# A four-layer block and a retrieval layer on one core: where the rows of the last 128 tokens are made, and how a gate becomes a row

## The chip, the cores and the metric

One NeuronCore of a Trainium2 chip runs the whole program. The metric is device time in microseconds; three executions of the kernel before took 2742.12 to 2751.5 us, median 2744.99. TensorE does matrix products, VectorE and ScalarE work on rows of 128 partitions, GpSimd (POOL) and SyncE (SP) here only issue DMAs. Profiled instructions are named by engine and by line of the kernel: L1447 is line 1447.

## The reference

512 tokens of width 1024 pass four mixer layers and then a block whose last part is a retrieval layer. All of the change lies in that part and in what follows it:

```
def peer_ffn(h, wq, sub_keys, expert_u, expert_v):          # h: (1, 512, 1024)
    ...
        q = (xb @ wq).reshape(PEER_BLOCK, PEER_HEADS, 2, PEER_HALF)
        s = jnp.einsum('thpd,hpkd->thpk', q, sub_keys)
        ...                                     # 8 heads choose 16 of 16,384 experts each
        g = jax.nn.softmax(best_s, axis=-1)
        act = jax.nn.gelu(jnp.einsum('thkd,td->thk', expert_u[experts], xb))
        wgt = g * act
        return jnp.einsum('thk,thkd->td', wgt, expert_v[experts])

    x = x + g2 * peer_ffn(h2, ...)              # g2: one gate of 1024 numbers for all tokens
    return rmsnorm_2(x, final_g)
```

## The kernel before

`peer()` computes this layer in two ways side by side. For tokens 0 to 319 it multiplies them by all 16,384 experts, 128 at a time: the *score part* `s_part()` (24 matmuls of 320 columns, lines 268 to 270 inside `gemm_t`, then a gelu on ScalarE, L1235) and, with the gates put in by VectorE (L1538), the *value part* `value_part()` (16 matmuls of 512 columns over three token blocks, L1483, L1484, L1486). Each of the 128 weights of `p_u` and of `p_v` (512 KB) is loaded by SP (L59), and split into a high and a low piece by ScalarE (L72, `whi`) and VectorE (L77, `wlo`). Raw weights have two or three buffers, split ones four.

For the other 192 tokens it gathers single experts' rows from DRAM: 64 tokens in halves (two partitions for each token, `two=True`) and the last 128 tokens one to a partition. POOL issues 384 gathers of 512 KB (L1456) into a ring of eight buffers. For a row of `p_u`, VectorE multiplies it with the token's normed row, kept in `hn` with one token on each partition, and sums (L1463); for a row of `p_v` it adds it with its weight to `ysum_h` or `ysum` (L1473). `hn` can hold one set of tokens: `hidden(True)` makes the 64 tokens' rows in front of the loop, and `hidden(False)` those of the last 128 when `consume()` has done the last product of the first kind. Both turn columns into rows by 16 matmuls with an identity (L1447) into two banks and two copies on ScalarE (L1448).

The last loop of `peer()` has 128 steps (L1525 on). A step loads the gates' columns `gr` (L1533, L1534), forms `wx` (L1538, L281, L282), consumes gathers, does a value part, for 21 <= i < 116 a score part for a later step, and issues up to four gathers by the table `CLOCK`. At i = 114 `last_rows()` makes `rw`, the two rows that the end needs on every partition: `final_g` by a broadcast DMA (L1491), and the gate `ada[:, 5]`, which lies in columns, by eight transposes into two banks (L1495) and two copies (L1496). `final(t)` multiplies a block's sums with the gate (L1515), adds the residual `y` (loaded at L1506, added at L1516), and norms it (L1518 to L1521). The value sums hold six of the eight PSUM banks through the loop, three of them in the pool of five whose other two serve all score parts, `hidden` and `last_rows`.

The code gives the order in which work is written down; a scheduler then orders the instructions of each engine by its own estimates, and an engine takes its list in order. So an edit in one place may move instructions in others. Loads of SP wait in SP's list in the same way, for a free buffer.

Of the kernel before, what the change touches and what calls it, by code (L numbers as in the profile page):

```python
# [10 lines left out]
F32 = mybir.dt.float32  # L11
# [3 lines left out]
AF = mybir.ActivationFunctionType  # L15
# [4 lines left out]
D = 1024  # L20
# [68 lines left out]
def program(ctx, tc, A, out, upto=99, dbg=None):  # L89
    nc = tc.nc  # L90
    V, SC, G, PE = nc.vector, nc.scalar, nc.gpsimd, nc.tensor
# [19 lines left out]
    dram = ctx.enter_context(tc.tile_pool(name="dram", bufs=1, space=bass.MemoryType.DRAM))  # L111

    def big(shape, dt, name):
        return bigp.tile(shape, dt, name=name, tag="big")

    def bank(shape=(128, S), pool="a"):
        return psp[pool].tile(list(shape), F32, name="bank" + pool, tag="bank" + pool)
# [4 lines left out]
    def tmp(shape, dt=F32, name="w2"):  # L122
        return w2.tile(shape, dt, name=name, tag="w2")
# [66 lines left out]
    ident = const.tile([128, 128], F32, name="ident")  # L190
# [716 lines left out]
    ada = const.tile([128, 6, KD], F32, name="ada")  # L907
# [294 lines left out]
    def peer(nrm, lp):  # L1202
# [6 lines left out]
        NG = ND // 32  # L1209
        gsp = dram.tile([32, 128, NG - 1, 128], F32, name="gsp")  # L1210
        gsl = dram.tile([32, 128, 128], F32, name="gsl")
        identr = lp.tile([128, 128], F32R, name="identr")
        V.tensor_copy(identr, ident)
        iota = lp.tile([128, 128], F32, name="iota")
# [88 lines left out]
        for m in range(16):  # L1303
# [8 lines left out]
            x = tmp([128, NT, 128])  # L1312
# [109 lines left out]
        hn = lp.tile([128, D], F32, name="hn")  # L1422
# [12 lines left out]
        def hidden(two):  # L1435

            for a in range(2):
                p = bank([128, 512])
                xs = [x[:, 4 * a:4 * a + 4, ND:ND + HALF] if two else x[:, 4 * a:4 * a + 4, ND + HALF:] for x in (nrm.h, nrm.l)]
                if two:  # L1440
                    twice = [tmp([128, 4, 2, HALF], F32R) for _ in xs]
                    for y, x in zip(twice, xs):
                        V.tensor_copy(y, x[:, :, None, :].to_broadcast([128, 4, 2, HALF]))
                    xs = [y.rearrange("p k a t -> p k (a t)") for y in twice]
                for k in range(4):
                    for i, x in enumerate(xs):
                        PE.matmul(p[:, k * 128:(k + 1) * 128], x[:, k], identr, start=i == 0, stop=i == 1)  # L1447
                SC.activation(hn[:, a * 512:(a + 1) * 512], p, AF.Copy)  # L1448
        act = lp.tile([128, 128], F32, name="act")
        ysum_h = lp.tile([128, D], F32, name="ysum_h")  # L1450
        order = [(two, p, n) for two in (True, False) for p in range(2) for n in range(HALF if two else 128)]
# [7 lines left out]
        def consume(two, p, n, u):  # L1459
            a, y, g = act[:, n:n + 1], ysum_h if two else ysum, gate_h if two else gate  # L1460
            last = g.shape[1] - 1
            if p == 0:
                V.tensor_tensor_reduce(u, u, hn, 1.0, 0.0, OP.mult, OP.add, a)  # L1463
                if n == last:
                    x = act[:, :last + 1]
                    SC.activation(x, x, AF.Gelu_apprx_tanh)
                    V.tensor_tensor(x, x, g, OP.mult)
                    if two:
                        hidden(False)
            elif n == 0:  # L1470
                V.tensor_scalar(y, u, a, None, OP.mult)
            else:
                V.scalar_tensor_tensor(y, u, a, y, OP.mult, OP.add)  # L1473
# [14 lines left out]
        def last_rows():  # L1488

            rw = big([128, 2, D], F32, "rw")  # L1490
            nc.sync.dma_start(rw[:, 1], A["final_g"].to_broadcast([128, D]))  # L1491
            for a in range(2):
                p = bank([128, 512])
                for k in range(4):
                    PE.transpose(p[:, k * 128:(k + 1) * 128], ada[:, 5, 4 * a + k:4 * a + k + 1].to_broadcast([128, 128]), ident)  # L1495
                SC.activation(rw[:, 0, a * 512:(a + 1) * 512], p, AF.Copy)  # L1496

            sel = lp.tile([128, 3 * HALF], F32, name="sel", tag="cand0")
            V.memset(sel, 0.0)
            V.tensor_tensor(sel[:, HALF:2 * HALF], ident[:, :HALF], ident[:, HALF:], OP.add)  # L1500
            return rw, sel

        def final(t):
# [18 lines left out]
            nc.sync.dma_start(out[0, t * 128:(t + 1) * 128], y[:, 1])  # L1522

        hidden(True)
        ring = [big([128, 4 * D], F32, "it") for _ in range(2)]  # L1525
        ring = [r[:, k * D:(k + 1) * D] for r in ring for k in range(4)]
        step, used, held, fetched = 0, 0, [], []
        clock = np.cumsum([CLOCK[(i >= MORE) + (i >= 128 - AHEAD)] for i in range(128)])
        for i in range(128):
# [16 lines left out]
            while fetched and fetched[0][0] <= i - LAG:  # L1546
                consume(*fetched.pop(0)[1:])
                used += 1
            if i == 114:
                rw, sel = last_rows()  # L1550
# [90 lines left out]
    if upto > 5:  # L1641
        with layer_pools(5) as lp:
            peer(nrm, lp)
# [119 lines left out]
```

## Time and profile before

| | before |
|---|---|
| median of three runs | 2744.99 us (2742.12 to 2751.5) |
| the profiled execution | 2749.09 us, of which the span from first to last instruction is 2747.0 us |
| TensorE, weight loads, VectorE, ScalarE, POOL busy | 95%, 81%, 79%, 47%, 20% of the span |
| moved by DMA | 653.67 MB, mean 238 GB/s |
| the last loop's DMA rate, slices 29 to 39 of 40 | 381 to 408 GB/s |

All rows come from the profiled execution. Times are microseconds from the start of its span. A busy time is the sum of an engine's instructions; a matmul's end is modelled, so it is the distance from one start to the next that tells how fast TensorE goes. Idle time is given with the instruction whose end finished it. `PEclk` is the clock granted to TensorE, as a share of the full one. "DMA" is the mean busy share of the 16 DMA engines; it can read a little over 1.

### The profile page before, as it was taken

Reading aid. Unit: us, or ns where it says so; the run is one execution under the profiler, and the core shown is the slowest. Engines: PE = TensorE matmul, PEld = TensorE weight load, DVE = VectorE, ACT = ScalarE, POOL = GpSimd, SP = SyncE. Lnnn points to the kernel's source line nnn. Section 1 sums busy time; section 2 is a strip of 40 time slices with the busy share of each in tenths; the row PEclk is TensorE's granted clock in tenths of the full one; section 3 lists DMA queues with packets and bytes.
Section 4 is the critical chain, followed back from the end, with each engine's and each line's share of the span. In section 5 each row is a group of like instructions: output and inputs, shape, how many; then the busy total and the mean of one; then the engine's idle time right before and its main releaser. Section 6 shows DMA issues by size and latency. Waiting matters only on the chain.

```text
span 2747.0 us, 40757 instructions
## 1 busy us (share of the span) xinstructions
PE 2610.9 (95%) x14379; PEld 2216.9 (81%) x14379; DVE 2174.8 (79%) x5296; ACT 1295.7 (47%) x2269; POOL 548.6 (20%) x431
## 2 busy tenths in 40 slices
PE   8999999999999999999999998889989999999988
PEld 7888888777767877897787788877879888888876
DVE  8975987756776777664435899788999899999998
ACT  5333455736775434445622346574444343444433
POOL 0000000000000000000000000005665666665661
PEclk9999999999999999999999999999999999999999
DMA  8773522142227886433345267779999999999996
GB/s 265 252 262 119 177 81 66 49 130 80 93 66 269 281 297 230 142 101 102 111 156 155 70 199 249 252 237 386 403 408 405 381 403 401 408 407 400 390 392 243
DMA packets 239788, 653.67 MB, mean 238 GB/s; under 512 B 23264, under 2 KB 80736, under 8 KB 239456
## 3 DMA queue, kind: packets, MB, share of 16 engines
q1 hardware_dynamic: 132640, 400.63, 41.7%
q0 software_dynamic: 61488, 223.90, 21.2%
q10 hardware_dynamic: 45456, 26.54, 3.3%
q8 instruction: 113, 1.85, 0.3%
q14 instruction: 91, 0.75, 0.1%
HBM read 583.29 MB, written 67.67 MB: 237 GB/s over the span
## 4 chain that ended last, share of the span: by engine, by line
PE 44%; DVE 22%; DMA 13%; issue 10%; POOL 5%; ACT 5%; ACTq 1%; SPq 0%; POOLq 0%; DVEq 0%
PE bankg L268 8%; PE bankg L269 8%; PE bankg L270 8%; POOL it L1456 5%; DVE wlo L77 4%; DMA wraw<-in_p_v_dram 3%; DMA wraw<-in_p_u_dram 3%; DVE ysum L1473 2%; PE bankg L428 2%; DVE it L1463 2%; PE bankg L430 2%; PE bankg L429 2%; DMA preraw<-in_p_u_dram 2%; PE bankg L543 2%; ACT whi L72 2%
## 5 line engine op out<-in xcount | busy, mean ns | idle before, releaser
L72 ACT ACTIVATE whi<-wraw 128x1024 fp32r<-128x1024 f32 (+1 forms) x491 | 515.3, 1051 | 806.0 <-PE bankg L269 220.6
L77 DVE TENSOR_TENSOR wlo<-wraw,whi 128x1024 fp32r<-128x1024 f32 (+2 forms) x448 | 541.3, 1209 | 206.1 <-ACT whi L72 199.6
L268 PE MATMUL bankg<-XH,whi 128*128 128x512 f32 x1032 | 408.9, 397 | 19.6 <-ACT whi L72 8.6
L270 PE MATMUL bankg<-XH,wlo 128*128 128x512 f32 x1032 | 405.3, 393 | 0.0
L269 PE MATMUL bankg<-XL,whi 128*128 128x512 f32 x1032 | 405.3, 393 | 0.0
L75 POOL DMA_DIRECT2D wlo<-lod x43 | 23.1, 538 | 1764.2 <-DVE vi L1319 1225.4
L268 PE MATMUL banka<-XH,whi 128*128 128x320 f32 x1024 | 320.8, 313 | 6.3 <-ACT whi L72 4.9
L270 PE MATMUL banka<-XH,wlo 128*128 128x320 f32 x1024 | 319.3, 312 | 4.6 <-DVE wlo L77 4.3
L269 PE MATMUL banka<-XL,whi 128*128 128x320 f32 x1024 | 317.6, 310 | 0.0
L268 PEld LDWEIGHTS bankg<-XH,whi 128*128 128x128 f32 x1032 | 195.7, 190 | 64.3 <-issue 11.9
L1463 DVE CUSTOM_DVE_ANT_0 it<-it,hn 128x1024 f32<-128x1024 f32 x192 | 229.9, 1217 | 6.9 <-DMA it<-in_p_urows_dram,idx 6.9
L270 PEld LDWEIGHTS bankg<-XH,wlo 128*128 128x128 f32 x1032 | 195.3, 189 | 41.3 <-DVE wlo L77 0.8
L269 PEld LDWEIGHTS bankg<-XL,whi 128*128 128x128 f32 x1032 | 195.5, 189 | 39.7 <-DVE XL L245 0.3
L268 PEld LDWEIGHTS banka<-XH,whi 128*128 128x128 f32 x1024 | 193.7, 189 | 13.6 <-ACT whi L72 5.1
L270 PEld LDWEIGHTS banka<-XH,wlo 128*128 128x128 f32 x1024 | 193.4, 189 | 8.6 <-DVE wlo L77 8.1
L1456 POOL DMA_INDIRECT it<-in_p_urows_dram,idx x128 | 179.9, 1406 | 94.1 <-DVE act L1463 71.4
L1456 POOL DMA_INDIRECT it<-in_p_v_dram,idx x128 | 173.8, 1358 | 113.7 <-DVE ysum L1473 102.4
L269 PEld LDWEIGHTS banka<-XL,whi 128*128 128x128 f32 x1024 | 193.6, 189 | 3.6
L428 PE MATMUL bankg<-whi,XH 128*128 128x256 f32 x576 | 165.1, 287 | 2.1 <-ACT XH L244 1.2
L430 PE MATMUL bankg<-whi,XL 128*128 128x256 f32 x576 | 164.1, 286 | 1.4 <-DVE XL L245 1.4
L429 PE MATMUL bankg<-wlo,XH 128*128 128x256 f32 x576 | 163.8, 285 | 0.0
L1473 DVE SCALAR_TENSOR_TENSOR ysum<-it,act,ysum 128x1024 f32<-128x1024 f32 x127 | 162.2, 1277 | 0.0
(513 smaller groups left out, 5835.5 us busy)
## 6 DMA issues: line engine op xcount, KB each, us to landing
wraw<-in_p_u_dram SPq DMA_DIRECT2D x128, 512.0 KB, 6.9
wraw<-in_p_v_dram SPq DMA_DIRECT2D x128, 512.0 KB, 7.2
wraw<-in_a_in_dram SPq DMA_DIRECT2D x64, 512.0 KB, 4.9
adaw<-in_ada_w_dram SPq DMA_DIRECT2D x48, 512.0 KB, 5.8
lod<-prelo SPq DMA_DIRECT2D x43, 512.0 KB, 5.9
wlo<-lod POOLq DMA_DIRECT2D x43, 512.0 KB, 5.5
gsp<-stage ACTq DMA_DIRECT2D x9, 2048.0 KB, 12.5
gr<-gsp SPq DMA_DIRECT2D x32, 576.0 KB, 8.3
```

The source lines that it names most:

```text
L72: nc.scalar.activation(h, t, AF.Copy)
L77: nc.vector.tensor_tensor(l, t, h.bitcast(F32), OP.subtract)
L268: PE.matmul(ps, a, xh[:, k, :], start=k == 0, stop=False)
L269: PE.matmul(ps, a, xl[:, k, :], start=False, stop=False)
L270: PE.matmul(ps, b, xh[:, k, :], start=False, stop=k == kk - 1)
L428: PE.matmul(ps, a, wh, start=k == 0, stop=False)
L429: PE.matmul(ps, a, wl, start=False, stop=False)
L430: PE.matmul(ps, b, wh, start=False, stop=k == len(blocks) - 1)
L543: PE.matmul(po[64 * a:64 * a + 64, b * 128:], v(m)[:, b, d:d + 64], xs[a][:, o:o + 128 * (NT - b)], start=b == 0, stop=b == 2)
L1456: G.indirect_dma_start(out=u, out_offset=None, in_=rows, in_offset=bass.IndirectOffsetOnAxis(ap=(idx_h if two else idx)[:, n:n + 1], axis=0))
L1463: V.tensor_tensor_reduce(u, u, hn, 1.0, 0.0, OP.mult, OP.add, a)
L1473: V.scalar_tensor_tensor(y, u, a, y, OP.mult, OP.add)
```

## The change

Two results are made in another place or way. First, `hidden(False)` is called right behind `hidden(True)`, in front of the loop. As `hn` still holds the 64 tokens' rows then, it copies its two halves into scratch tiles and SP stores them to a DRAM tile `hnd`. Where `consume()` called it, POOL now loads `hn` from `hnd`. Second, the gate row is not made by transposes: SP writes the columns of `ada[:, 5]` as one row to a DRAM tile `gate_row` at the start of `peer()`, and `last_rows()` loads it onto all partitions by a broadcast DMA.

```
+        hnd = dram.tile([128, D], F32, name="hnd")
+        gate_row = dram.tile([1, D], F32, name="gate_row")
+        nc.sync.dma_start(gate_row.rearrange("o (k p) -> p (o k)", p=128), ada[:, 5])
...
-                SC.activation(hn[:, a * 512:(a + 1) * 512], p, AF.Copy)
+                x = hn[:, a * 512:(a + 1) * 512] if two else tmp([128, 512])
+                SC.activation(x, p, AF.Copy)
+                if not two:
+                    nc.sync.dma_start(hnd[:, a * 512:(a + 1) * 512], x)
...
                     if two:
-                        hidden(False)
+                        nc.gpsimd.dma_start(hn, hnd)
...
-            for a in range(2):
-                p = bank([128, 512])
-                for k in range(4):
-                    PE.transpose(p[:, k * 128:(k + 1) * 128], ada[:, 5, 4 * a + k:4 * a + k + 1].to_broadcast([128, 128]), ident)
-                SC.activation(rw[:, 0, a * 512:(a + 1) * 512], p, AF.Copy)
+            nc.sync.dma_start(rw[:, 0], gate_row.to_broadcast([128, D]))
...
         hidden(True)
+        hidden(False)
```

Line numbers of the changed kernel are higher by three to six behind the first new lines: L1463 is L1469 there, L1538 is L1541, L1483 is L1489.

Beside the edited lines the scheduler orders three places anew. The first is VectorE at the start of the last loop; `w_...` are scratch tiles, the rows ahead of the first gather product are shown. Before:

```order
L77 TENSOR_TENSOR wlo<-wraw,whi 128x1024 x2
L282 TENSOR_TENSOR wx<-w_18408,wx 128x320
L282 TENSOR_TENSOR wx<-w_18455,wx 128x320
L1538 TENSOR_TENSOR w_18583<-sgb,gr 128x320
L77 TENSOR_TENSOR wlo<-wraw,whi 128x1024
L1538 TENSOR_TENSOR w_18630<-sgb,gr 128x320
L1538 TENSOR_TENSOR w_18672<-sgb,gr 128x320
L1538 TENSOR_TENSOR w_18707<-sgb,gr 128x320
L1538 TENSOR_TENSOR w_18744<-sgb,gr 128x320
L1463 ISA it,act<-it,hn 128x1024
L1463 ISA act 128x1
```

and with the change:

```order
L1431 COPY gr<-stage 128x128
L77 TENSOR_TENSOR wlo<-wraw,whi 128x1024 x6
L1469 ISA it,act<-it,hn 128x1024
L1469 ISA act 128x1
L1469 ISA it,act<-it,hn 128x1024
L1469 ISA act 128x1
L1469 ISA it,act<-it,hn 128x1024
L1469 ISA act 128x1
L1541 TENSOR_TENSOR w_18298<-sgb,gr 128x320
L1260 CAST w_18326<-vi 128x256
L1541 TENSOR_TENSOR w_18350<-sgb,gr 128x320
L282 TENSOR_TENSOR wx<-w_18298,wx 128x320
```

Before, all of the first steps' products L1538 stand ahead of the first gather product (L1463), and so does the end of `choose(TD)`, some 30 rows higher. Now six splits of weights (L77) and three gather products (L1469) stand ahead of the first of either.

The second is TensorE at i = 114, at the end of a score part. Before:

```order
L268 MATMUL banka<-XH,whi 128x320
L269 MATMUL banka<-XL,whi 128x320
L270 MATMUL banka<-XH,wlo 128x320
L1495 MATMUL banka<-ident,ada 128x128 x4
L1483 MATMUL bankg<-whi,wx 128x512
L1484 MATMUL bankg<-wlo,wx 128x512
L1486 MATMUL bankg<-whi,wx 128x512
L1483 MATMUL bankg<-whi,wx 128x512
```

and with the change:

```order
L268 MATMUL banka<-XH,whi 128x320
L269 MATMUL banka<-XL,whi 128x320
L270 MATMUL banka<-XH,wlo 128x320
L1489 MATMUL bankg<-whi,wx 128x512
L1490 MATMUL bankg<-wlo,wx 128x512
L1489 MATMUL bankg<-whi,wx 128x512
L1492 MATMUL bankg<-whi,wx 128x512
```

The four transposes between score part and value part are gone, and so are four more behind the value part's fourth matmul. The last two score parts, which before stand behind 163 further value matmuls in the list, now follow within 16 value matmuls each.

The third is SP at the end of the loop. Before:

```order
L59 DMA wraw<-in_p_v_dram 128x1024 x3
L1533 DMA gr<-gsp 128x1152
L1534 DMA gr<-gsl 128x128
L59 DMA wraw<-in_p_v_dram 128x1024 x9
L1491 DMA rw<-in_final_g_dram 128x1024
L1506 DMA y<-x_14423 128x1024 x4
L1522 DMA out_dram<-y 128x1024 x4
```

and with the change:

```order
L59 DMA wraw<-in_p_v_dram 128x1024 x3
L1536 DMA gr<-gsp 128x1152
L1537 DMA gr<-gsl 128x128
L59 DMA wraw<-in_p_v_dram 128x1024 x2
L1497 DMA rw<-in_final_g_dram 128x1024
L1498 DMA rw<-gate_row 128x1024
L59 DMA wraw<-in_p_v_dram 128x1024
L1508 DMA y<-x_14423 128x1024
L59 DMA wraw<-in_p_v_dram 128x1024 x2
L1536 DMA gr<-gsp 128x1152
L1537 DMA gr<-gsl 128x128
L59 DMA wraw<-in_p_v_dram 128x1024 x4
```

The loads of `rw` (now two) and the first of `y` stood behind the last weight and now stand in front of seven and of six weights. The buffers for `rw` and for the first `y` are those of the normed columns `XH` and `XL`, which the last score part reads.

## Rows read from the trace of the kernel before

**Rows 1.** the page, section 1 and the DMA row of section 2 (tenths)
```profile
PE 2610.9 (95%) x14379; PEld 2216.9 (81%) x14379; DVE 2174.8 (79%) x5296; ACT 1295.7 (47%) x2269; POOL 548.6 (20%) x431
...
DMA  8773522142227886433345267779999999999996
```

**Rows 2.** stretches: start:end, length, busy us (count) by engine, PEclk, DMA, GB/s
```profile
1872.00:1890.00 18.00, 17.73 (x77) 14.21 (x77) 17.76 (x29) 6.33 (x12) 11.59 (x8) 1.00 1.04 404
...
2020.00:2040.00 20.00, 11.66 (x56) 10.24 (x55) 18.30 (x20) 8.46 (x14) 10.37 (x10) 0.74 1.03 408
...
2040.00:2140.00 100.00, 100.00 (x552) 89.83 (x551) 95.90 (x99) 41.43 (x69) 59.88 (x46) 1.00 1.03 406
...
2140.00:2160.00 20.00, 20.00 (x114) 18.11 (x114) 15.91 (x18) 5.82 (x9) 11.11 (x9) 1.00 0.88 335
...
2160.00:2660.00 500.00, 487.01 (x2620) 427.26 (x2618) 470.33 (x619) 203.59 (x329) 318.36 (x229) 1.00 1.02 401
...
2660.00:2680.00 20.00, 13.95 (x62) 11.35 (x61) 19.41 (x22) 7.99 (x14) 12.56 (x10) 0.83 1.01 386
...
2700.00:2720.00 20.00, 20.00 (x105) 17.34 (x104) 19.74 (x23) 9.59 (x17) 1.22 (x1) 1.00 0.60 212
```

**Rows 3.** waits in 1880 to 2740: us in total, times, longest us
```profile
ACT whi L72 <- DMA wraw<-in_p_v_dram: 196.3, 95, 8.3
...
ACT whi L72 <- DMA wraw<-in_p_u_dram: 133.6, 70, 5.1
```

**Rows 4.** TensorE's rows: start, length, line, tiles, count [idle <- who], 2021 to 2040
```profile
2021.90 0.31 PE L270 MATMUL banka<-XH,wlo 128*128 128x320 f32 x1
...
2025.80 0.33 PE L1447 MATMUL banka<-identr,XH 128*128 128x128 f32 x1 [3.58 <-ACT sgb L1235]
...
2036.55 0.40 PE L1483 MATMUL bankg<-whi,wx 128*128 128x512 f32 x1
...
2038.87 0.31 PE L268 MATMUL banka<-XH,whi 128*128 128x320 f32 x1
...
2039.74 0.31 PE L268 MATMUL banka<-XH,whi 128*128 128x320 f32 x1
```

**Rows 5.** stretches at the mid-loop stop, columns as in rows 2
```profile
2026.00:2036.00 10.00, 5.25 (x21) 4.67 (x21) 10.00 (x11) 4.61 (x9) 5.48 (x5) 0.51 1.03 410
```

**Rows 6.** TensorE's rows at the stop ahead of the tail
```profile
2662.20 0.31 PE L270 MATMUL banka<-XH,wlo 128*128 128x320 f32 x1
...
2670.14 1.12 PE L1495 MATMUL banka<-ident,ada 128*128 128x128 f32 x4 [5.37 <-ACT sgb L1235]
...
2675.53 0.39 PE L1483 MATMUL bankg<-whi,wx 128*128 128x512 f32 x1
```

**Rows 7.** VectorE's rows at the start of the last loop
```profile
1842.20 0.49 DVE L1538 TENSOR_TENSOR w<-sgb,gr 128x320 f32<-128x320 f32 x1 [2.86 <-DMA gr<-gsp]
...
1850.56 0.23 DVE L1562 TENSOR_SCALAR idx<-ei 128x128 int32<-128x128 int32 x1
...
1872.03 1.23 DVE L77 TENSOR_TENSOR wlo<-wraw,whi 128x1024 fp32r<-128x1024 f32 x1 [0.42 <-ACT whi L72]
...
1874.78 1.22 DVE L1463 CUSTOM_DVE_ANT_0 it<-it,hn 128x1024 f32<-128x1024 f32 x1
```

**Rows 8.** TensorE's row of the first value matmul
```profile
1868.63 0.45 PE L1483 MATMUL bankg<-whi,wx 128*128 128x512 f32 x1
```

**Rows 9.** TensorE's row of the last value matmul
```profile
2730.91 0.40 PE L1484 MATMUL banka<-wlo,wx 128*128 128x512 f32 x1
```

**Rows 10.** VectorE's rows behind the last gather: its next and its last
```profile
2716.04 1.22 DVE L77 TENSOR_TENSOR wlo<-wraw,whi 128x1024 fp32r<-128x1024 f32 x1
...
2741.80 1.28 DVE L1521 SCALAR_TENSOR_TENSOR y<-y,rs_yb,rw 128x1024 f32<-128x1024 f32 x1
```

**Rows 11.** SyncE's queue: the first load of rw
```profile
2708.90 0.33 SPq L1491 DMA_DIRECT2D rw<-in_final_g_dram  x1
```

## The prediction

> **What bounds the kernel now.** I read the page first, then the table of stretches, then the waits of the last loop, and then single rows where TensorE stands. By the page TensorE is busy 95% of the span [rows 1], but that is a mean over all stages. What the change touches lies in the last loop, from 1868.6 us [rows 8] to the end, so its stretches decide [rows 2]. The reader is to see three nearly full resources there. The DMA engines stand at a share of 1.01 to 1.04 and 386 to 408 GB/s from 1872 on, but for 2140 to 2160 (0.88, 335). VectorE works 470.33 of the 500 us from 2160. TensorE's busy time is modelled, so I count matmuls instead: a step is 16 matmuls of the value part at 0.232 us (ten of them lie between 2036.55 and 2038.87 [rows 4]) and 24 of the score part at 0.146 (six between 2038.87 and 2039.74, with rounding), 7.2 us for 40. The 552 matmuls of 2040 to 2140 make 99.4 of 100 us: TensorE is at its peak. The 2620 of 2160 to 2660 make 472 of 500: it is starved for about 5%, though its busy time reads 487.
>
> By the Trainium skill ("Perfetto Trace Analysis", Identifying the Most-Contended Engine) a matmul's busy share is a poor measure of the distance from the peak, and the busy share of the weight loads a better one. By the former (97%) TensorE would set the pace; by the latter, 427 us where the peak of 89.83 per 100 would be 449, it is starved for 5%, as the count says.
>
> Who starves it is seen in the waits [rows 3]: ScalarE's split of a weight (L72) waits 196.3 and 133.6 us for weights to land. So over the long stretch the DMA engines pace the loop, and TensorE only here and there.
>
> **What goes: the stop in mid-loop.** The 16 matmuls of L1447 stand behind a score part whose bank ScalarE has not emptied; the first starts at 2025.80 after 3.58 us of idle time [rows 4], and then the granted clock is 0.51 in 2026 to 2036 [rows 5], the lower of its levels. Between the start of the last score matmul before it (2021.90) and that of the next score part (2038.87) lie 16.97 us, with one value part of 16 x 0.232 = 3.7 us in them. TensorE loses 13.3 us. **The stop ahead of the tail** is alike: eight transposes (L1495) in two banks, the second four after 5.37 us of idle time; from 2662.20 to 2675.53 are 13.3 us for one value part [rows 6]. It loses 9.6. Together 22.9.
>
> What is late next there? Without L1447 a value part comes first, which needs no new bank and takes 3.7 us; the next score part needs the bank that ScalarE gives free at 2025.80, 3.9 us after 2021.90. So nearly all of the stop goes.
>
> But is it on the path? During the first stop the DMA engines ran at 1.03 and 408 GB/s [rows 2], so what paces the loop lost nothing. Behind it TensorE is at its peak until 2140 and starved again from 2160: the buffers (four split weights, two or three raw ones) had swallowed the 13 us. I cost that gain at nothing. Behind the second stop TensorE doesn't recover; it runs to its last value matmul at 2730.91 [rows 9]. But VectorE works 19.41 and 19.74 of 20 us around the tail [rows 2], and its last row ends the span but for the store [rows 10]. So a gain there counts only as far as VectorE's list behind the last gather gets shorter.
>
> **What is added.** The normed rows go to DRAM and back, 0.52 + 0.52 MB: at 408 GB/s 2.6 us of the DMA engines. The write stands on SP's queue behind six weights and ahead of reloads for step 12 and later; the read on POOL's queue between two gathers, where it waits for the last product of the first kind, while the ring's gathers behind it wait for VectorE's same row anyway: nothing. One load of `rw` and the first of `y` went out at 2708.90 and later [rows 11], where the DMA engines are at 0.60 [rows 2]; now SP issues them, and the second load of `rw`, among the last nine weights, in the saturated stretch: 3 x 0.52 = 1.57 MB, 3.8 us. VectorE's new order at the change of gather kind may spare the dip of 2140 to 2160: (408 - 335) / 408 x 20 = 3.6 us. In all 2.6 + 3.8 - 3.6 = +2.8 us of DMA time.
>
> By the Trainium skill ("DMA: Bandwidth & Descriptors", Issuing engines are not separate DMA queues) loads from SP and POOL share the same 16 engines; the trace agrees, with 408 GB/s as the most that both queues reach. Were POOL's queue a path of its own, the read back would be free and the sum +1.5. The rule speaks against a trip by DRAM in this loop: by it alone, with nothing won on TensorE, the time would be 2745 + 2.8 = 2748, the upper edge of the forecast's own range.
>
> SP's write of 1,024 single elements, about 1,065 us into the span by its place in SP's order, has no row of its kind. From below it costs nothing: the page's slice there, the sixteenth (1030 to 1099 us), shows DMA at 6 tenths [rows 1], and the row isn't read for another 1,600 us. From above it holds the two weight loads behind it for one stop like those of rows 4, 3.6 us. I take 0, as that slice is far from the 9 tenths of the last loop.
>
> **What moves** is the start of the loop. Before, VectorE did the rest of `choose(TD)` and four products L1538 from 1842.20 to 1850.79, then eight more L1538 and five L282 between the first six L77, and the first gather product at 1874.78 [rows 7]; the first value part began at 1868.63 [rows 8]. Now six L77 stand first, of which the last ran until 1873.3 [rows 7]; three gather products of 1.2 us; two L1538, a cast and L282, 1.6 us: the first value part comes at about 1878.5, up to 2 us earlier if weights land earlier, as SP now issues six of them ahead of four reloads of 0.16 MB. TensorE loses 8 to 10 us, I take 9. And 8.6 + 13 x 0.45 = 14 us of VectorE's work move into the loop; it has 30 us idle in the long stretch alone [rows 2]. The first gather product itself comes 1.5 us earlier, so the ring of eight gathers doesn't stop sooner. DMA time lost: 0, if the gathers fill the gap, to 4 us, the weights' share of 9 (in the long stretch 229 gathers [rows 2] go with 2620 / 40 x 2 = 131 weights, 0.36 of the loads; rounded up).
>
> **Sum.** The last gather lands 2.8 to 6.8 us later. Behind the last gather's sum VectorE needs 27 us (2716.04 to 2743.1 [rows 10]); two L77, two L1538 and two L282 of these, 4.4 us, now stand ahead of it. And the eight gathers of the ring, 10 us of VectorE's work when the last one landed, may be less behind with TensorE not stopped: 0 to 8 us. So from 2.8 - 4.4 - 8 = -9.6 to 6.8 - 4.4 = +2.4, the middle -3.6. The sum is made against the profiled 2749.09: 2745.5. That execution lies 4.1 above the median of 2744.99 in all its parts as far as I can tell, so I take the difference over to the median: **2741**.
>
> **The rivals.**
> *TensorE sets the pace.* For it: its peak in 2040 to 2140, and the value matmuls in a row to 2730.91. Then 22.9 - 9 = 14 us are won: 2731. Against it: 472 of 500 us.
> *The late start decides.* If the raw weights and the ring are full before VectorE's first gather product, the DMA engines stand until the first value part frees a buffer, 9 us that a saturated loop can't make good, and 2.8 of the bytes: 2745 + 11.8 = 2757. It decides once loads stop for more than about 5 us after 1872. Against it: 404 GB/s in 1872 to 1890 [rows 2], with VectorE's first product at 1874.78.
> *The change doesn't do what it says at the tail:* SP holds `rw` until the last score part frees its buffer, seven weights behind it, and the stop comes back as a wait for weights: 5.4 us once more [rows 6], 2750.
>
> **How the numbers follow.** Forecast 0.47 (2741, its own range 2735 to 2748), TensorE sets the pace 0.25 (2731), late start 0.20 (2757), held queue 0.08 (2750). What a measurement of this kernel can tell from no change is about 0.3%, 8.2 us: below 2736.8 is faster, above 2753.2 slower. Faster: 0.25 and 0.05 of the forecast's lower edge, 0.30. Slower: 0.18 and 0.02, 0.20. Within: 0.50. The range, 2730 to 2757, leaves out about 0.1 on each side.
>
> **What would show it.** Right: no idle time over 1 us of TensorE at the two places, and a count of matmuls behind the first that now falls short of the peak; the DMA share as before; the first value part near 1878; the last gather 3 to 7 us later, and VectorE's rows behind its sum near 22 us. Wrong: a loop that ends 14 us earlier with more than 408 GB/s (TensorE paced), a hole in the DMA share between 1872 and 1890 (late start), or a wait for weights behind `rw`.

## The result, and the profile after

The change makes the kernel slower: 1.0069 of the time before (95% interval 1.0054 to 1.0085); medians 2762.9 and 2744.99 us. 2741 was forecast, 2730 to 2757 the range. One of the seven executions of the change took 7164.13 us and is left out of the ratio. The profiled execution's span is 2756.1 us, 9.1 longer than that of before; it was the fastest of the six others, so the profile shows less of the loss than the medians do.

The page of the kernel after; the rows answer to [rows 1]:

```profile
span 2756.1 us, 40696 instructions
...
PE 2611.6 (95%) x14371; PEld 2215.4 (80%) x14371; DVE 2172.1 (79%) x5296; ACT 1300.1 (47%) x2267; POOL 561.9 (20%) x432
...
DMA  7773522132227896433344267779999999999996
```

TensorE and VectorE do the same work as before (their busy times differ by less than 3 us) in a longer span. The stretches of the last loop, with the columns of [rows 2] (start:end, length, then TensorE, weight loads, VectorE, ScalarE, POOL busy with counts, clock, DMA share, GB/s):

```profile
1872.00:1890.00 18.00, 14.61 (x52) 11.73 (x53) 15.38 (x38) 7.00 (x15) 7.76 (x6) 0.75 0.98 331
1890.00:1950.00 60.00, 59.55 (x256) 47.61 (x255) 57.72 (x122) 25.45 (x45) 29.29 (x22) 1.00 1.01 383
1950.00:2020.00 70.00, 70.00 (x376) 61.99 (x375) 64.35 (x102) 28.59 (x47) 42.47 (x31) 1.00 1.01 388
2020.00:2040.00 20.00, 20.00 (x111) 17.95 (x110) 18.84 (x29) 8.51 (x15) 14.70 (x11) 1.00 1.03 407
2040.00:2140.00 100.00, 98.22 (x534) 86.29 (x532) 95.92 (x99) 42.11 (x66) 60.40 (x46) 1.00 1.03 408
2140.00:2160.00 20.00, 18.53 (x104) 16.44 (x103) 18.98 (x21) 7.74 (x12) 12.97 (x9) 1.00 1.03 408
2160.00:2660.00 500.00, 481.48 (x2597) 422.13 (x2596) 472.52 (x620) 204.68 (x327) 332.34 (x231) 1.00 1.02 402
2660.00:2680.00 20.00, 19.84 (x107) 17.34 (x106) 20.00 (x22) 8.69 (x13) 13.57 (x10) 1.00 1.03 407
2680.00:2700.00 20.00, 13.40 (x56) 10.47 (x55) 14.65 (x17) 5.46 (x10) 9.24 (x9) 0.91 1.03 409
2700.00:2720.00 20.00, 17.46 (x74) 13.47 (x73) 19.41 (x24) 7.91 (x15) 7.42 (x6) 1.00 0.95 358
```

Three of these stretches before, which [rows 2] leave out:

```profile
1890.00:1950.00 60.00, 59.71 (x256) 47.77 (x255) 54.70 (x88) 27.14 (x46) 30.43 (x25) 1.00 1.03 405
1950.00:2020.00 70.00, 69.48 (x380) 61.54 (x378) 69.32 (x109) 28.97 (x49) 50.77 (x35) 1.00 1.03 405
...
2680.00:2700.00 20.00, 20.00 (x87) 16.11 (x86) 19.36 (x20) 7.46 (x12) 10.45 (x10) 1.00 1.03 406
```

Three things are to be seen. The mid-loop stop is gone (2020 to 2040: 20.00 us busy, 11.66 before), the clock stays at 1.00 there (0.74 before), and the next stretch now counts 534 matmuls instead of 552: TensorE is starved at once, as forecast. The start is worse: 331 GB/s in 1872 to 1890 (404 before), with the granted clock at 0.75 behind TensorE's wait for its first value part, then 383 and 388 where 405 was measured before. Against those rates the three stretches miss 73 x 18 + 22 x 60 + 17 x 70 = 3.8 MB, 9.4 us at 405 GB/s. And the tail is no longer full: TensorE's 13.40 of 20 us in 2680 to 2700 and 17.46 in 2700 to 2720, both 20.00 before.

**The start**, VectorE's rows ahead of the loop, which answer to [rows 7], and TensorE's first value matmul, which answers to [rows 8]:

```profile
1840.02 0.23 DVE L1431 COPY gr<-stage 128x128 f32<-128x128 f32 x1 [1.57 <-ACT stage L1408]
...
1855.45 2.36 DVE L77 TENSOR_TENSOR wlo<-wraw,whi 128x1024 fp32r<-128x1024 f32 x2 [15.20 <-ACT whi L72]
```

```profile
1875.39 0.80 PE L1489 MATMUL bankg<-whi,wx 128*128 128x512 f32 x1 [6.59 <-ACT wx L281]
```

VectorE stands idle for 15.20 us, from 1840.2 to 1855.45, for the first weight's high piece. There, before, it did the rest of `choose(TD)` and four products (1842.20 to 1850.79). The first value matmul comes 19.9 us behind the first split (1855.45) instead of 11.7 (1856.89 to 1868.63). The rest of `choose(TD)` now ends at 1951.3, among the gather products, and POOL's gathers of 1872 to 1950 wait for it (us in total, times, longest; L1292 and L1294 are lines of `choose`, and no such wait is there before):

```profile
POOL it L1462 <- DVE best L1294: 8.7, 5, 2.5
...
POOL it L1462 <- DVE best L1292: 3.6, 2, 2.5
```

**The store of the gate's row**, by its line (count, durations; then us from issue to landing, min, median, max), SP's list around it, the split that waited on ScalarE, and the stretch:

```profile
L1214 SPq DMA_DIRECT2D gate_row<-ada x1: 433/433/433, 1055.9 to 1055.9; - x1
...
DMA to landing us min/median/max: 11.2/11.2/11.2
```

```profile
1055.48 0.33 SPq L59 DMA_DIRECT2D wraw<-in_a_out_dram  x1
1055.86 0.43 SPq L1214 DMA_DIRECT2D gate_row<-ada  x1
1057.21 0.34 SPq L59 DMA_DIRECT2D wraw<-in_a_out_dram  x1
```

```profile
1067.04 1.06 ACT L72 ACTIVATE whi<-wraw 128x1024 fp32r<-128x1024 f32 x1 [11.35 <-DMA wraw<-in_a_out_dram]
```

```profile
1060.00:1065.00 5.00, 5.00 (x23) 4.14 (x23) 0.49 (x1) 0.00 (x0) 0.00 (x0) 1.00 0.70 29
```

4 KB took 11.2 us to land. The weight for which ScalarE waited 11.35 us is the one issued 0.38 us ahead of the store: it landed after 11.5 us, and the one issued behind the store after 12.7. Before, the same two loads took 4.3 and 4.7. In that stretch the DMA engines were busy for 0.70 and moved 29 GB/s.

**The tail**: SP's queue, which answers to [rows 11], two splits of weights on ScalarE, and TensorE's idle times:

```profile
2681.95 0.33 SPq L1497 DMA_DIRECT2D rw<-in_final_g_dram  x1
...
2682.33 0.43 SPq L1498 DMA_DIRECT2D rw<-gate_row  x1
...
2684.24 0.33 SPq L59 DMA_DIRECT2D wraw<-in_p_v_dram  x1
...
2684.62 0.43 SPq L1508 DMA_DIRECT2D y<-x  x1
```

```profile
2685.57 1.06 ACT L72 ACTIVATE whi<-wraw 128x1024 fp32r<-128x1024 f32 x1 [4.52 <-DMA wraw<-in_p_v_dram]
...
2696.49 1.06 ACT L72 ACTIVATE whi<-wraw 128x1024 fp32r<-128x1024 f32 x1 [6.65 <-DMA wraw<-in_p_v_dram]
```

```profile
2689.60 0.53 PE L1489 MATMUL bankg<-whi,wx 128*128 128x512 f32 x1 [3.79 <-ACT wx L281]
...
2697.96 0.50 PE L1489 MATMUL bankg<-whi,wx 128*128 128x512 f32 x1 [2.82 <-ACT wx L281]
```

The loads of `rw` and `y` are in the queue around the weight issued at 2684.24. It landed after 12.2 us (7.1 is the median of these weights) and is split only at 2696.49, after 6.65 us of waiting. ScalarE's list is in order, so L281 of the next `wx` stands behind that split, and TensorE, whose value part needs `wx`, is idle 2.82 us. The 3.79 us ahead of that are not those loads' alone: they stand behind weights that SP issued at 2677.58 and next, ahead of `rw`, which landed after 7.9 and 8.2 us. The stop of [rows 6] is gone from its place, and one of 6.6 us stands some 20 us later.

The streams of the loop, read from the starts of VectorE's rows (nth gather consumed, nth split of a weight from 1830 us on), in us:

| | gather 0 | gather 24 | gather 240 | gather 383 | weight 16 | weight 208 | weight 224 |
|---|---|---|---|---|---|---|---|
| before | 1874.8 | 1926.6 | 2396.0 | 2714.8 | 1917.7 | 2657.7 | 2719.0 |
| after, less before | -3.9 | +13.2 | +19.3 | +14.8 | +4.6 | -1.5 | +9.2 |
| e2 (rows only), less before | +0.9 | +17.0 | +21.2 | +15.7 | +8.5 | +1.3 | +14.6 |
| e9 (rows, `choose` ahead), less before | -6.4 | +3.4 | +0.6 | -7.1 | +0.9 | -12.9 | -8.3 |

The weights are on time again by the loop's end, up to the tail. The gathers fall 17 us behind within the first 24 and stay there.

### The profile page after: what moved, and what is told of

Read it like the earlier page. It is cut to its first block, busy times and chain, and to the rows that moved or that the text cites. A ratio compares the mean times of both kernels' runs of the same rounds, so it can differ in the third digit from the quotient of the medians.

```text
span 2756.1 us, 40696 instructions
## 1 busy us (share of the span) xinstructions
PE 2611.6 (95%) x14371; PEld 2215.4 (80%) x14371; DVE 2172.1 (79%) x5296; ACT 1300.1 (47%) x2267; POOL 561.9 (20%) x432
## 3 DMA queue, kind: packets, MB, share of 16 engines
q0 software_dynamic: 61632, 224.42, 21.2%
## 4 chain that ended last, share of the span: by engine, by line
PE 47%; DVE 27%; DMA 15%; issue 5%; ACT 5%; ACTq 0%; SPq 0%; DVEq 0%
PE bankg L268 7%; DMA wraw<-in_p_u_dram 7%; PE bankg L269 7%; PE bankg L270 7%; DVE wlo L77 5%; DVE it L1469 3%; DVE ysum L1479 2%; PE bankg L428 2%; PE bankg L430 2%; PE bankg L429 2%; DMA preraw<-in_p_u_dram 2%; ACT whi L72 2%; PE bankg L543 2%; DMA wraw<-in_p_v_dram 1%; PE banka L1407 1%
## 5 line engine op out<-in xcount | busy, mean ns | idle before, releaser
L77 DVE TENSOR_TENSOR wlo<-wraw,whi 128x1024 fp32r<-128x1024 f32 (+2 forms) x448 | 541.2, 1209 | 226.4 <-ACT whi L72 218.6
L1469 DVE CUSTOM_DVE_ANT_0 it<-it,hn 128x1024 f32<-128x1024 f32 x192 | 228.3, 1217 | 0.6 <-ACT hn L1452 0.6
L1462 POOL DMA_INDIRECT it<-in_p_urows_dram,idx x128 | 186.4, 1456 | 90.6 <-DVE act L1469 61.4
L1489 PE MATMUL bankg<-whi,wx 128*128 128x512 f32 x384 | 155.7, 405 | 27.6 <-ACT wx L281 27.6
L1492 PE MATMUL bankg<-whi,wx 128*128 128x512 f32 x384 | 154.8, 407 | 9.6 <-DVE wx L282 9.0
```

Source lines behind the costliest of these rows:

```text
L77: nc.vector.tensor_tensor(l, t, h.bitcast(F32), OP.subtract)
L1462: G.indirect_dma_start(out=u, out_offset=None, in_=rows, in_offset=bass.IndirectOffsetOnAxis(ap=(idx_h if two else idx)[:, n:n + 1], axis=0))
L1489: PE.matmul(po[a][b], parts[0], w[0][:, ds], start=i == 0, stop=False)
L1492: PE.matmul(po[a][b], parts[1], w[0][:, ds], start=False, stop=i == 127)
```

## The experiments

All ratios are to the kernel before on the same chip, with 95% intervals. Theory A holds three local costs responsible; its rivals are the start alone (B), TensorE as the pace (C), the DRAM trip (D).

**e1, e2, e3: the parts alone.** e1 has only the diff's lines on `gate_row` and `rw`, e2 only those on `hnd` and `hidden`, e3 only the store:

```
+        gate_row = dram.tile([1, D], F32, name="gate_row")
+        nc.sync.dma_start(gate_row.rearrange("o (k p) -> p (o k)", p=128), ada[:, 5])
```

> The kernel before with only the gate's row by way of DRAM; the normed rows stay in mid-loop. Theory A (three local costs: the element-wise write holds a weight in the layer near 1060 us; two scratch tiles spoil the loop's start; rw and y are loaded ahead of the last weights): the start of the loop is as before (first value matmul 0 to 8 us later only because of the write), the mid-loop stop is there, the stop at L1495 is gone but TensorE stands for 3 to 10 us among the last seven value parts. Time 2745 + 5 (write) + (-5 to +5): 2745 to 2755. Theory B (the loop's start alone makes the change slow): 2738 to 2745, since a stop is gone and the start is as before.

> The kernel before with only the rows made ahead of the loop and kept in DRAM; the gate still by transposes. Theory A: first value matmul 6 to 8 us later than before, VectorE idle for about 15 us ahead of its first weight, the gather products about 13 us later from the 24th on, mid-loop stop gone, stop at L1495 still there: 2752 to 2760. Theory B: nearly all of the 18 us, 2757 to 2765. Theory C (TensorE paces the loop, the edit is good and the gate's part spoils it): 2735 to 2742.

> The kernel before plus the element-wise store of the gate's row, which nothing reads. Theory A: the store takes about 11 us to land, a weight's split behind it waits about as long, and whatever stands behind 1075 us comes 4 to 8 us later: 2749 to 2753. Theory B: hidden by the loads in flight, 2745 +- 2.

Measured: e1 1.0033 (1.0015 to 1.0050), e2 1.0074 (1.0050 to 1.0097), e3 1.0029 (1.0012 to 1.0046). B falls: the start is not the only cost. In e3's trace the store lands like this; the weight issued behind it lands after 11.9 us, and its split waits:

```profile
DMA to landing us min/median/max: 11.3/11.3/11.3
```

```profile
1076.99 1.06 ACT L72 ACTIVATE whi<-wraw 128x1024 fp32r<-128x1024 f32 x1 [6.69 <-DMA wraw<-in_a_out_dram]
```

What stands behind this place on SP, the first store of the next layer's columns, in the kernel before and in e3:

```profile
1089.71 0.43 SPq L986 DMA_DIRECT2D xd<-X  x1
```

```profile
1097.36 0.42 SPq L986 DMA_DIRECT2D xd<-X  x1
```

Up to 1057 us the two executions were level (SP's issues 0.3 us apart), here e3 is 7.7 us late. The store alone costs what the whole gate part costs, so that at the tail the lost stop and the earlier loads cancel out, within some 7 us by the two intervals.

**e4, e5: the rows without scratch tiles.** The rows made ahead of the loop are put in `ysum_h`, which is idle until the first sum. e4 copies them to `hn` on ScalarE (the fourth line below); e5 takes the change's trip by DRAM, with its store to `hnd` (the last).

```
+                x = (hn if two else ysum_h)[:, a * 512:(a + 1) * 512]
+                SC.activation(x, p, AF.Copy)
...
-                        hidden(False)
+                        SC.activation(hn, ysum_h, AF.Copy)
+                        nc.gpsimd.dma_start(hn, hnd)
```

> The rows are made ahead of the loop as in the change, but put in ysum_h (idle until the first sum of the first kind) instead of scratch tiles and DRAM; one ScalarE copy brings them to hn. Gate by transposes as before. Theory A: VectorE's order at the start is that of before again; start as before, mid-loop stop gone, and as DMA paces little is won: 2740 to 2745. Theory C (TensorE paces): 13 us won, 2731 to 2734. If the place of the work and not the scratch tiles makes the start late: 2752 or more.

> As e4_rows_ysum, but ysum_h's content goes to DRAM and POOL loads hn from there, as in the change: the change's move with its DRAM trip, without the two scratch tiles. Theory A (the scratch tiles make the start late): VectorE's order at the start as before, 2744 plus at most 2.6 for 1.05 MB of a saturated loop: 2744 to 2748. Theory D (the DRAM trip itself, by its bytes or by its wait on POOL's queue, is the cost of e2_rows_only): 2755 or more.

Measured: e4 1.0007 (0.9995 to 1.0019), e5 1.0002 (0.9985 to 1.0019). VectorE's order at the start is that of before in both. Two scratch tiles of the change, not its place nor its DRAM trip, make the rows part cost 20 us (e2). D falls. And C falls: in e4 the mid-loop stop is gone,

```profile
2020.00:2040.00 20.00, 19.77 (x102) 16.56 (x101) 19.28 (x20) 8.44 (x13) 12.38 (x10) 1.00 1.03 409
2040.00:2140.00 100.00, 98.93 (x540) 87.28 (x539) 95.89 (x100) 42.20 (x68) 62.07 (x46) 1.00 1.03 406
```

with 19.77 of 20 us busy where 11.66 were, and nothing is won: 1.0007, and the next 100 us count 540 matmuls instead of 552.

**e9: what of the late start costs.** As e2, with the scratch tiles, but `choose(TD)` is written out ahead of the rows:

```
         _, steps = choose(TD)
+        while steps:
+            steps.pop(0)()
+        V.tensor_scalar(idx, ei, 16383, None, OP.bitwise_and)
```

> As e2_rows_only (scratch tiles and DRAM trip kept), but the rest of choose(TD) is written ahead of the rows, so that VectorE does it in the 15 us in which it stands idle in e2; the products L1538 stay behind three gather products. If e2's loss is VectorE's moved work: about half of the 20 us comes back (choose is 7 of 14 us), 2752 to 2758. If it is the late first value part, 6 us behind before: nothing comes back, 2762 to 2768.

Measured: 0.9992 (0.9974 to 1.0009). All of e2's loss comes back, more than expected. VectorE's idle time ahead of its first split, in e2 and in e9, and e9's first value matmul:

```profile
1860.45 2.36 DVE L77 TENSOR_TENSOR wlo<-wraw,whi 128x1024 fp32r<-128x1024 f32 x2 [14.34 <-ACT whi L72]
```

```profile
1853.83 2.36 DVE L77 TENSOR_TENSOR wlo<-wraw,whi 128x1024 fp32r<-128x1024 f32 x2 [8.77 <-ACT whi L72]
```

```profile
1872.87 0.80 PE L1491 MATMUL bankg<-whi,wx 128*128 128x512 f32 x1 [5.69 <-ACT wx L281]
```

The first value matmul is still 19.0 us behind the first split, as in the change (19.9). So TensorE's late start costs nothing that the timed runs show. What cost is the work of `choose`, taken out of a wait and strewn among the gather products; the products L1538 stand behind three gather products in e9 too, and that costs nothing either. The stretches 1890 to 1950 and 1950 to 2020 of e2, then of e9:

```profile
1890.00:1950.00 60.00, 60.00 (x258) 48.26 (x257) 58.38 (x121) 26.17 (x44) 29.43 (x22) 1.00 1.01 383
1950.00:2020.00 70.00, 70.00 (x373) 61.68 (x372) 64.73 (x107) 28.62 (x47) 42.23 (x31) 1.00 1.01 392
```

```profile
1890.00:1950.00 60.00, 60.00 (x258) 48.26 (x258) 55.72 (x90) 24.16 (x45) 26.99 (x23) 1.00 1.03 402
1950.00:2020.00 70.00, 70.00 (x381) 62.48 (x380) 67.27 (x107) 30.13 (x49) 46.26 (x32) 1.00 1.03 406
```

VectorE has 58.38 us of work in the first 60 of e2, 55.72 in e9; POOL has issued 64 gathers by 2020 us in e2 and 71 in e9 (74 before), and the DMA engines move 383 instead of 402 GB/s at nearly the same share.

**e6, e10: the gate part without the element-wise store.** e6 turns the eight columns by one transpose and stores eight runs of 512 bytes; e10 also holds the loads of `rw` and of the first `y` back by copies of one or two elements on VectorE (the last two lines below) that must wait for the `wx` of step 121 and of step 125, and calls `last_rows()` at step 121 instead of 114.

```
+        PE.transpose(p[:8], ada[:, 5], ident)
+        SC.activation(x[:8], p[:8], AF.Copy)
+        nc.sync.dma_start(gate_row.rearrange("o (k p) -> (o k) p", p=128), x[:8])
...
+            V.tensor_copy(rw[:, :, 0], x.bitcast(F32)[:, :2])
+                V.tensor_copy(y[:, 0, :1], held[0][1][0].bitcast(F32)[:, :1])
```

> As e1_gate_only, but the gate's columns are turned by one transpose at the start of the last layer and stored as 8 runs of 512 bytes instead of 1,024 single elements. Theory A: no stop near 1060 us, the tail as in e1, where what the lost stop gives and the earlier loads take are about equal: 2744 to 2748. If the tail's loads were the cost of e1: 2752 to 2756.

> As e6_gate_t, with the loads of rw and of the first y held until behind seven and nine of the last nine weights, as in e8. If the loads ahead of the weights eat what the lost stop at the tail gives: 2738 to 2742, 3 to 6 below e6. If nothing is to be had at the tail: 2743 to 2746.

Measured: e6 1.0007 (0.9988 to 1.0026), e10 0.9972 (0.9957 to 0.9988). With the store made in eight runs e1's loss is gone. And the loads ahead of the weights eat what the lost stop gives: SP's load of `rw` and TensorE's idle times behind it, in e6 and then in e10:

```profile
2680.95 0.42 SPq L1496 DMA_DIRECT2D rw<-in_final_g_dram  x1
```

```profile
2700.34 0.50 PE L1488 MATMUL bankg<-whi,wx 128*128 128x512 f32 x1 [4.26 <-ACT wx L281]
...
2702.57 0.79 PE L1491 MATMUL bankg<-whi,wx 128*128 128x512 f32 x1 [1.49 <-DVE wx L282]
```

```profile
2694.58 0.33 SPq L1497 DMA_DIRECT2D rw<-in_final_g_dram  x1
```

```profile
2695.47 0.50 PE L1488 MATMUL bankg<-whi,wx 128*128 128x512 f32 x1 [0.97 <-ACT wx L281]
2696.50 0.50 PE L1491 MATMUL bankg<-whi,wx 128*128 128x512 f32 x1 [0.30 <-DVE wx L282]
...
2711.54 0.73 PE L1488 MATMUL bankg<-whi,wx 128*128 128x512 f32 x1 [2.03 <-ACT wx L281]
```

5.75 us of idle time at this place became 1.27, with 2.03 more 15 us later. From the last load of `p_u` (2658.19 and 2656.02) to the end of the span are 86.0 us in e6 and 83.1 in e10, 85.3 before. By the timed runs the held loads are worth 0.0035, 9.6 us; with the two intervals, which touch, that is 3 to 16. e10 has the lowest ratio of the study, 0.28% below the kernel before.

**e7, e8, e11: both parts mended.** e7 is e4 and e6 together; e8 and e11, one kernel, are e7 with e10's held loads.

> e4_rows_ysum and e6_gate_t together: both stops gone, no element-wise store, no scratch tiles, no DRAM trip for the rows. Theory A (DMA engines pace): 2740 to 2746. Theory C (TensorE paces): 2722 to 2732.

> As e7_both, but one-element copies on VectorE hold the loads of rw until step 121's wx and of the first y until step 125's, so that SP issues them behind seven and nine of the last nine weights. If loads ahead of the last weights make TensorE and VectorE wait there (as the change's profile shows, 9 us of idle time): 3 to 6 below e7_both, 2735 to 2741. If the tail is VectorE's own work: the same as e7_both.

> e8_both_late once more, for its interval against the kernel before: 0.995 to 0.999 of it if the gain of e8 (0.9987) is real; 0.999 to 1.001 if it was chance.

Measured: e7 0.9991 (0.9975 to 1.0008), e8 0.9987 (0.9966 to 1.0008), e11 0.9981 (0.9963 to 0.9999). With both stops gone TensorE has 23 us less to lose, and the time hardly moves: C falls again. Whether the held loads help here can't be told from e7, e8 and e11.

**e12, e13, e14: the whole change, with one cause or all taken out.** e12 has e9's edit, e13 e6's, e14 both and e10's.

> The whole change, with only the rest of choose(TD) written ahead of the rows. If the two costs add and each is what e2/e9 and e3 showed: the start's part goes, the element-wise store's 8 us stay, the tail as in e1: 1.002 to 1.004 of the kernel before (2750 to 2756). If the change's start costs less than e2's, as the sum of e1 and e2 (1.0107) over the change (1.0069) may mean: the same 1.003, with only 10 us won over the change.

> The whole change, with only the element-wise store replaced by one transpose and 8 runs of 512 bytes (as e6). If the start's cost in the change is e2's 20 us and the store's its 8: 1.007 (2764). If the store took 8 of the change's 18 us: 1.004 (2755), and the start costs 10 there, less than in e2, where the transposes at the tail are still in the way.

> The whole change with all three mended: choose(TD) ahead of the rows, one transpose for the store, the loads of rw and the first y held behind the last weights. Scratch tiles and both DRAM trips stay. 0.996 to 0.999 (2734 to 2742), as e10 and e11, if nothing else in the change costs.

Measured: e12 1.0043 (1.0029 to 1.0056), e13 1.0039 (1.0020 to 1.0058), e14 0.9994 (0.9981 to 1.0008). With all three mended the change is as fast as the kernel before, with its scratch tiles and DRAM trips still in it; 0.996 to 0.999 was expected of it, so the gain of e10 isn't seen there. Each of the two large causes is worth some 0.3% here. In the rows part alone the start was worth 0.7 to 0.8%; why it is less in the whole change isn't settled. e2's tail, where the transposes and the two score parts put off behind them meet the late gathers, is the place to look: by then e2 is 1.3 us late by its weights, and 14.6 at the last.

## Why the prediction was wrong, point by point

Three terms of its sum failed: the DMA time lost at the start, the element-wise store, and the loads ahead of the last weights.

**Right: both stops go from their places, and the first is worth nothing.** The DMA engines paced the loop behind it (e4 1.0007), the count of matmuls fell as soon as the stop was gone. The dip of 2140 to 2160 went as forecast (335 to 408 GB/s). The DRAM trip's 2.6 us were not seen (e5 1.0002), but its interval, up to 1.0019, leaves room for them.

**Right in size: the first value part's delay.** 8 to 10 us, up to 2 less with earlier weights; measured 19.9 - 11.7 = 8.2 behind the first split, 6.8 on the span's clock.

**Wrong: what moves.** The prediction saw 14 us of VectorE's work go into the loop and set against it 30 us of idle time *in the long stretch*, from 2160 on. But the work lands between 1874 and 1952, where VectorE's list is full (57.72 of 60 us in 1890 to 1950 now, 54.70 before), and where an engine's list is in order a product that comes later frees its ring buffer later. Behind it VectorE has less to do than before (64.35 of 70 us in 1950 to 2020, 69.32 before), as fewer gathers come. "DMA time lost: 0 to 4 us" was 9.4 by the rates above; the last gather was consumed 14.8 us later, not 2.8 to 6.8. The term should have been priced at the place where the work goes: 14 us against what is idle up to the first step that has room. e9 shows that it was this term, and of its 14 us the part of `choose`, and not the late value part.

**Wrong: the element-wise store, taken as 0, at most 3.6.** Measured 7.7 us at its place, 0.29% in e3. The prediction took its 0 from how busy the DMA engines were in the slice (6 tenths). Its bound had the right victims, weights, but only those behind the store, and the price of another stop: in the change the load ahead of the store and the one behind it both landed some 7 to 8 us later than before, and ScalarE waited 11.35 us. By the Trainium skill ("DMA: Bandwidth & Descriptors", Rules for kernel authors) a strided last dimension becomes one descriptor per element; the trace agrees, with packets under 512 bytes up from 23264 to 24304 in e3, for one store of 1,024 elements. The bound from above should have been a landing time for that many pieces.

**Mis-sized: the tail.** The loads of `rw` and `y` ahead of the weights were priced by their bytes, 3.8 us. e10 against e6 is 0.0035, 9.6 us (3 to 16): a weight behind them lands 5 us later than the median, ScalarE's list stands behind its split, and TensorE and VectorE behind that. So what the second stop gave was taken again: e6 1.0007. That the stop of [rows 6] was 9.6 us too proves nothing, with such an interval, and in the change itself part of the new stop stands behind weights issued ahead of these loads: this term's size is the least certain of the three. This is the rival "held queue" (0.08) with another wait: SP's queue was hardly held (`rw` went out at 2681.95), the loads themselves were in the way. VectorE's rows behind the last gather were sized well: from the end of that gather's sum at 2730.9 to 2752.0 are 21 us, 22.6 were forecast.

**The rival of the slower side** named the start, with 2757, but not the mechanism: in e9 the first value part is as late and nothing is lost. Its price, 2757, came nearer to the measured 2763 than the forecast by luck: it had one cost that is not there and lacked the three that are.

**The base.** The prediction carried the difference over to the median as if the profiled execution were slow in all its parts. By the splits' starts it lost some 3 us between 2534 and 2658 that other executions did not lose (e4's offset to it goes from -0.9 to -4.4 there, e12's from -0.3 to -3.5). So part of the 4.1 us was lost at one place. That moves no verdict.

## What to carry to other kernels

Where an engine takes its list in order, price moved work at the place where it lands: idle time elsewhere doesn't pay for it, and work that stood in a wait was free only there. Two scratch tiles more can turn the order of a whole stretch, so look who else allocates from that pool, and put a result that must wait in a tile that is idle anyway. Price a DMA by what is in flight beside it and by its pieces, not by its bytes: a 4 KB store of single elements cost 8 us (0.29%, 0.12 to 0.46), and 1.57 MB moved ahead of late weights took about what the stop that it replaced had given.

## What the runs showed that was not expected

A store of 4 KB in 1,024 pieces takes 11.2 to 11.3 us to land (after, e3), longer than a 512 KB weight takes in the saturated loop (6.9 and 7.2 by the page of before). Single executions differ by up to 11 us at the same place of a layer that no edit touches: SP's last early load of `p_u` (1046.9 us before) is issued 7.2 us earlier in the profile of the change, 8.0 earlier in e5, 3.0 later in e2. So spans of two profiles can't be compared closer than that, and an offset in the table above is to be read against the column next to it and not by itself; the ratios come from the timed runs.
